# The taps of a depthwise convolution: from split diagonals to plain fp32 products on 32x32 parts of the array

## The chip, the cores and the metric

The kernel runs on one core of one Trainium2 chip. The metric is the device time of one execution in microseconds, given as the median of several runs. The engines are named as the profile names them: PE is TensorE's matmul, PEld its weight load, DVE is VectorE, ACT is ScalarE, POOL is GpSimd, SP is SyncE. A DMA queue is marked by a q behind the engine that issues to it.

## The reference, cut to what matters

A decoder trunk of two layers, 512 tokens by 1024 features, all in float32. Layer 0 has a mixer of state-space groups and attention, layer 1 a convolution module. In both layers a residual, a layer norm, an MLP and another layer norm follow. The change lies in the convolution module of layer 1:

```python
def conformer_conv(x, w_pw1, b_pw1, w_dw, b_dw, ln_g, ln_b, w_pw2, b_pw2):
    h = x @ w_pw1 + b_pw1
    val, gate = jnp.split(h, 2, axis=-1)
    h = val * jax.nn.sigmoid(gate)
    h = lax.conv_general_dilated(                    # depthwise, causal, 31 taps
        h, w_dw[:, None, :], window_strides=(1,), padding=[(CONV_SIZE - 1, 0)],
        dimension_numbers=('NWC', 'WIO', 'NWC'), feature_group_count=CONV_WIDTH) + b_dw
    h = jax.nn.silu(layer_norm(h, ln_g, ln_b))
    return h @ w_pw2 + b_pw2
```

and, around it, `x = layer_norm(alpha * x + mix)`.

## The kernel before

Activations lie with features on the partitions and tokens along the row: a tensor of 1024 features is eight tiles of 128 x 512. The tokens are also cut into two halves of 256 columns (half 0 and half 1), so that a layer norm of one half can run while PE works on the other.

**Products.** A float32 product is made of three products in the type fp32r: both operands are split into a high part and a rest (hi, lo), and hi x hi, hi x lo and lo x hi are summed in PSUM (`gemm`, L219 to L227). The split is one cast on ScalarE and one subtraction on VectorE (`split`, L214 to L217). A few products are plain fp32; each of those shows as two records in the trace, so `colmean` (L873), which makes one product for a mean and four for a variance, shows two records (mpc) and eight (vpc) for each half.

**The convolution stage** (L1041 to L1135) goes through eight tiles of 128 features, j = 0 to 7.
- `glu_tile(j)` makes value and gate (pv and pg, 24 products each; those of tiles 0 and 1, called pl, are made before the stage), the sigmoid on ScalarE (csg), and the gated product on VectorE (hp), behind 30 columns of zeros. hp is split too (hph, hpl).
- `taps_pe(j)` does the first taps on PE: for each tap ScalarE builds two 128 x 128 diagonal matrices from the identity (dh and dl, the hi and lo part of that tap's weights), and PE makes three products of them with a shifted window of hph and hpl, summed in one PSUM bank (cv). PE_TAPS says how many taps: 2, 6, 8, 9, 11, 14 for tiles 0 to 5, and for the halves of tiles 6 and 7 13, 14 and 13, 8.
- `taps_dve(j)` does the other taps: ScalarE opens two sums with the last two taps (cy, cz), and VectorE adds one tap in each step, cy and cz in turn (L1090, recorded as L357). At the end cz and cv are added to cy (recorded as L353).
- `LN.add` sums the tiles as they come (sc, L871); `LN.norm` makes the mean (mpc), subtracts it, squares (sqc on ScalarE), makes the variance (vpc) and its reciprocal root (rc). Then every tile is scaled, passed through Silu and split (csh, csl).
- The tail (`tail_norm_lead`, `Tail`) multiplies the eight split tiles with w_pw2 (tld, 24 products for a half tile), adds the residual and makes the next norm (mpd, vpd). The lead (fl) is the first part of the MLP behind it.

Tiles 6 and 7 are worked in halves, in the order of the list TAIL: P is `taps_pe`, V `taps_dve`, G `glu_tile` for half 1, N the norm of a half; the two digits are tile and half.

**What sets the order.** A scheduler orders the instructions of each engine by the order in which the program makes them and by what is ready, and puts in the semaphores. `tc.add_manual_dep` with NOSYNC fixes the order of two instructions on one engine; in this stage that is used for little. PSUM has six banks for products (`nps`) and two for statistics (`stp`). Weights come through `Weights`: those of the convolution and the tail were split in layer 0 and kept in DRAM, and come back by POOL's DMA queue, each into a slot that waits for PE to have used what is in it; `W.ahead` says how many are asked for in advance.

Of the kernel before, what the change touches and what calls it, by code (L numbers as in the profile page):

```python
# [9 lines left out]
F32 = mybir.dt.float32  # L10
F32R = mybir.dt.float32r
# [154 lines left out]
def kernel(ctx: ExitStack, tc: tile.TileContext, a: dict, out: bass.AP):  # L166
# [639 lines left out]
    def nps(name):  # L806
        return nps_.tile([P, T], F32, tag="n", name=name)
# [7 lines left out]
    def tmp(name, dt=F32):  # L815
        return hid.tile([P, T], dt, tag="tmp", name=name, bufs=8)
# [43 lines left out]
    class LN:  # L860
# [4 lines left out]

        def add(self, j, ys, c0, c1):

            if j == 1:
                self.s[c0] = tmp(f"s{self.n}{c0}")[:, c0:c1]
            if j:  # L870
                (V if j == KT - 1 or self.n in LN_ON_V else G).tensor_tensor(self.s[c0], ys[0][:, c0:c1] if j == 1 else self.s[c0], ys[j][:, c0:c1], op=ALU.add)  # L871

        def colmean(self, srcs, c0, c1, nm, other):  # L873

# [98 lines left out]
            W.fence = None  # L973
            return [ps for _, ps in self.held]

    def tail_norm_lead(xk, name, bias, g, b, lead_n, lead_name):

        ln = LN(name)
        t = Tail(xk, ln, bias)
        t.run(KT)  # L980
# [35 lines left out]
    wdh = hid.tile([P, KT, CONV], F32R, tag="wdh", name="wdh")  # L1016
    wdl = hid.tile([P, KT, CONV], F32, tag="wdl", name="wdl")
# [12 lines left out]
    k0 = 0  # L1030
    for bi, nb in enumerate(FFN_BLOCKS[0]):
# [8 lines left out]

    acc = [None] * KT  # L1041
    hps = [None] * KT
    cps = [None] * KT

    def glu_tile(j, c0=0, c1=T):
        if c0 == 0:
            if j < 2:
                ps[j] = first[2 * j : 2 * j + 2]
            else:
                ws[j], ps[j] = (W.next(), W.next()), (nps(f"pv{j}"), nps(f"pg{j}"))  # L1050
            hps[j] = hpage(f"hp{j}", F32, PAD + T), hpage(f"hph{j}", F32R, PAD + T), hpage(f"hpl{j}", F32R, PAD + T)
# [6 lines left out]
        hp, hh, hl = hps[j]  # L1058
        p0 = PAD + c0 if c0 else 0
# [3 lines left out]
        split(hh[:, p0 : PAD + c1], hl[:, p0 : PAD + c1], hp[:, p0 : PAD + c1])  # L1063

    def taps_pe(j, c0=0, c1=T):
        _, hh, hl = hps[j]
        if c0 == 0:
            cps[j] = nps(f"cv{j}")
        n = PE_TAPS[c0 > 0][j]
        for t in range(n):  # L1070
            dh = hid.tile([P, P], F32R, tag="dh", name=f"dh{j}{t}", bufs=DBUFS)
            dl = hid.tile([P, P], F32R, tag="dl", name=f"dl{j}{t}", bufs=DBUFS)
            act(dh, ident, AF.Copy, scale=wdh.bitcast(F32)[:, j, t : t + 1])
            act(dl, ident, AF.Copy, scale=wdl[:, j, t : t + 1])
            for i, (u, v) in enumerate(((dh, hh), (dh, hl), (dl, hh))):
                PE.matmul(cps[j][:, c0:c1], u, v[:, t + c0 : t + c1], start=t == 0 and i == 0, stop=t == n - 1 and i == 2)  # L1076

    def taps_dve(j, c0=0, c1=T):

        hp = hps[j][0]  # L1080
        if c0 == 0:
            acc[j] = page(f"cy{j}", F32), hpage(f"cz{j}", F32)
        y, z = (x[:, c0:c1] for x in acc[j])
        t = CONV - 1
        act(y, hp[:, t + c0 : t + c1], AF.Identity, bias=pv("conv_b_dw", j), scale=wdw[:, j, t : t + 1])
        t = CONV - 2
        opened = act(z, hp[:, t + c0 : t + c1], AF.Copy, scale=wdw[:, j, t : t + 1])
        for i, t in enumerate(range(CONV - 3, PE_TAPS[c0 > 0][j] - 1, -1)):
            o = (y, z)[i % 2]
            stt(o, hp[:, t + c0 : t + c1], wdw[:, j, t : t + 1], o, ALU.mult, ALU.add)  # L1090
        tt(y, y, z, ALU.add)
        tt(y, y, cps[j][:, c0:c1], ALU.add)
        return opened

    ln = LN("c")
    n = KT - SPLIT_TILES
    cs_, ws, ps = None, [None] * KT, [None] * KT
    glu_tile(0)
    glu_tile(1)
    taps_pe(0)  # L1100
    for j in range(n):
        if j + 2 < KT:
            W.ahead = AHEAD[j + 2 >= n]
            glu_tile(j + 2, 0, T if j + 2 < n else H)
        if j + 1 < n:
            taps_pe(j + 1)
        opened = taps_dve(j)
        if j == 1:
            with tc.issue_after(opened):
                for i in range(KT):  # L1110
                    act(X[i], X[i], AF.Identity, bias=rb[2][:, i : i + 1], scale=ALPHA)
        for c0, c1 in HALVES:
            ln.add(j, [x and x[0] for x in acc], c0, c1)
    for o in TAIL:
        j, (c0, c1) = int(o[1]), HALVES[int(o[-1])]
        if o[0] == "P":
            taps_pe(j, c0, c1)
        elif o[0] == "V":
            taps_dve(j, c0, c1)
            ln.add(j, [x and x[0] for x in acc], c0, c1)  # L1120
        elif o[0] == "G":
            glu_tile(j, H, T)
        else:
            ys = [x[0] for x in acc]
            r = ln.norm(ys, c0, c1)
            cs_ = cs_ or new_x("cs")
            for j in range(KT):
                y = ys[j][:, c0:c1]
                tt(y, y, r, ALU.mult)
                act(y, y, AF.Silu, bias=pv("conv_ln_b", j), scale=pv("conv_ln_g", j))  # L1130
                done = split(cs_[j][0][:, c0:c1], cs_[j][1][:, c0:c1], y)
                if c0 == 0 and j == FJ:
                    W.fence = done
    W.ahead = AHEAD[0]
    xs, first = tail_norm_lead(cs_, "d", None, ("ln1_g", 8), ("ln1_b", 8), LEAD, "fl1")  # L1135


    XT = [None] * KT
# [106 lines left out]
```

## Time and profile before

| | |
|---|---|
| median of 3 runs | 1217.15 us (1216.98 to 1217.62) |
| profiled execution: its own time | 1217.5 us |
| its span in the trace | 1215.8 us |
| granted TensorE clock, mean | 0.995 |
| busy: PE, DVE, ACT, POOL | 98%, 65%, 46%, 5% of the span |
| chain that ended last, by engine | PE 83%, DVE 10%, ACT 4%, DMA 2%, issue 1% |
| convolution stage | about 667 us to 823 us of the span |
| tap products on PE (L1076) | 98 x 3: 150 of 512 columns, 144 of 256 |

The page's first part gives busy time, share of the span and number of instructions of each engine. A view by stretches gives the same for pieces of the span. The chain of waits is followed back from the last instruction: at each step to what released it, or to the instruction before it on its engine; its rows are start, length and what ran, with a count. A group of instructions is written as out<-in with the program's own names, partitions x elements, count, then busy time, mean nanoseconds of one, idle time before them and what ended it. A matmul's duration is longer than the distance to the next, since they are pipelined; the pace is read from the chain, as length over count.

### The profile page before, as it was taken

What the parts mean: (1) busy time and instruction counts of PE and PEld (TensorE: products, weight loads), DVE (VectorE), ACT (ScalarE), POOL (GpSimd) and SP (SyncE); (2) the same over time, 40 slices, a digit from 0 to 9 for tenths busy, and PEclk for the clock granted to TensorE, in tenths of its full rate; (3) what the DMA queues carried; (4) which work ended last, traced back from release to release, by engine and by line L of the source; (5) the groups of instructions that cost most, each with busy time, mean ns of one, the idle gap of its engine ahead of it and who ended that gap; (6) DMA issues with size and microseconds to landing.
All of it is one profiled execution on the core that took longest, in us unless ns stands there. A gap on an engine that the chain in (4) does not pass through costs nothing.

```text
span 1215.8 us, 16751 instructions
## 1 busy us (share of the span) xinstructions
PE 1187.4 (98%) x6546; PEld 1007.5 (83%) x6546; DVE 786.9 (65%) x1400; ACT 557.1 (46%) x990; POOL 58.2 (5%) x125
## 2 busy tenths in 40 slices
PE   9899999999999999999999999899999999999997
PEld 7677776789988888888999888889988888888885
DVE  7998774578745635646566999998843443434446
ACT  6836665734525524425323456964651332323230
POOL 1001101100000000000022110102000000000000
PEclk9999999999999999999999999999999999999999
DMA  8510042150878787887454631406142232323211
GB/s 205 155 49 22 19 130 61 31 195 1 264 250 282 251 284 264 270 283 268 165 183 159 213 104 36 139 1 208 39 152 87 87 108 83 122 70 121 70 52 69
DMA packets 128943, 168.86 MB, mean 139 GB/s; under 512 B 11298, under 2 KB 101666, under 8 KB 128864
## 3 DMA queue, kind: packets, MB, share of 16 engines
q1 hardware_dynamic: 120064, 136.30, 34.5%
q0 software_dynamic: 8640, 31.46, 7.6%
q8 instruction: 51, 0.84, 0.3%
q14 instruction: 28, 0.23, 0.1%
q10 hardware_dynamic: 160, 0.03, 0.0%
HBM read 132.12 MB, written 35.65 MB: 138 GB/s over the span
## 4 chain that ended last, share of the span: by engine, by line
PE 83%; DVE 10%; ACT 4%; DMA 2%; issue 1%; POOL 0%; SPq 0%; DVEq 0%; POOLq 0%; ACTq 0%
PE f L225 23%; PE g L1175 12%; PE acf L225 11%; PE fl L225 5%; PE tld L225 4%; PE tlb L225 4%; PE h L1159 3%; PE cv L1076 2%; PE pv L225 2%; PE pg L225 2%; PE tla L225 2%; PE pl L225 2%; DVE cz L357 1%; PE acmo L225 1%; PE av L709 1%
## 5 line engine op out<-in xcount | busy, mean ns | idle before, releaser
L102 DVE TENSOR_TENSOR wlo<-raw,whi 128x1024 fp32r<-128x1024 f32 x176 | 213.4, 1224 | 199.5 <-ACT whi L101 198.7
L101 ACT CAST whi<-raw 128x1024 fp32r<-128x1024 f32 x176 | 182.1, 1049 | 313.5 <-PE g L1175 107.4
L1175 PE MATMUL g<-whi,hh 128*128 128x512 f32 x208 | 81.8, 393 | 0.0
L1175 PE MATMUL g<-wlo,hh 128*128 128x512 f32 x208 | 81.8, 393 | 0.0
L1175 PE MATMUL g<-whi,hl 128*128 128x512 f32 x208 | 81.7, 393 | 0.0
L225 PE MATMUL f<-xah,whi 128*128 128x512 f32 x208 | 81.2, 390 | 0.0
L225 PE MATMUL f<-xdl,whi 128*128 128x512 f32 x208 | 81.1, 390 | 0.0
L225 PE MATMUL f<-xah,wlo 128*128 128x512 f32 x208 | 81.0, 390 | 0.0
L225 PE MATMUL f<-xdh,whi 128*128 128x512 f32 x208 | 81.0, 390 | 0.0
L225 PE MATMUL f<-xal,whi 128*128 128x512 f32 x208 | 81.0, 390 | 0.0
L225 PE MATMUL f<-xdh,wlo 128*128 128x512 f32 x208 | 81.0, 390 | 0.0
L225 PE MATMUL acf<-hl,whi 128*128 128x512 f32 x192 | 75.7, 394 | 0.0
L225 PE MATMUL acf<-hh,wlo 128*128 128x512 f32 x192 | 75.6, 394 | 0.0
L225 PE MATMUL acf<-hh,whi 128*128 128x512 f32 x192 | 75.5, 393 | 0.0
L215 ACT CAST hh<-fr 128x512 fp32r<-128x512 f32 x64 | 39.7, 621 | 59.6 <-DVE fr L353 59.6
L216 DVE TENSOR_TENSOR hl<-fr,hh 128x512 fp32r<-128x512 f32 x64 | 44.1, 690 | 31.9 <-ACT hh L215 31.8
L357 DVE SCALAR_TENSOR_TENSOR cy<-hp,wdw,cy 128x512 f32<-128x512 f32 (+1 forms) x99 | 63.6, 654 | 0.2
L357 DVE SCALAR_TENSOR_TENSOR cz<-hp,wdw,cz 128x512 f32<-128x512 f32 (+1 forms) x93 | 60.0, 656 | 0.0
L353 DVE TENSOR_TENSOR fr<-fr 128x512 f32<-128x512 f32 x64 | 43.7, 685 | 14.7 <-ACT fr L154 14.6
L1175 PEld LDWEIGHTS g<-wlo,hh 128*128 128x128 f32 x208 | 39.1, 188 | 8.9
L1175 PEld LDWEIGHTS g<-whi,hl 128*128 128x128 f32 x208 | 39.1, 188 | 8.9
L1175 PEld LDWEIGHTS g<-whi,hh 128*128 128x128 f32 x208 | 39.1, 188 | 8.8
(684 smaller groups left out, 3093.4 us busy)
## 6 DMA issues: line engine op xcount, KB each, us to landing
raw<-in_ffn_w_dram SPq DMA_DIRECT2D x48, 1024.0 KB, 5.8
raw<-in_ffn_w_dram SPq DMA_DIRECT2D x32, 512.0 KB, 3.5
kepth<-whi SPq DMA_DIRECT2D x30, 512.0 KB, 8.6
keptl<-wlo SPq DMA_DIRECT2D x30, 512.0 KB, 9.4
whi<-kepth POOLq DMA_DIRECT2D x30, 512.0 KB, 3.7
wlo<-keptl POOLq DMA_DIRECT2D x30, 512.0 KB, 4.5
raw<-in_conv_w_pw_dram SPq DMA_DIRECT2D x12, 1024.0 KB, 6.5
raw<-in_mix_w_in_dram SPq DMA_DIRECT2D x16, 512.0 KB, 3.9
```

The source lines that it names most:

```text
L101: i0 = nc.scalar.copy(hi, raw).ins
L102: i1 = nc.vector.tensor_sub(lo, raw, hi.bitcast(F32)).ins
L215: i0 = S.copy(hi, src).ins
L216: i1 = V.tensor_sub(lo, src, hi.bitcast(F32)).ins
L225: ins = PE.matmul(ps[:, c0:c1], u[:, k, ksl], v[:, c0:c1], start=start and k == 0 and i == 0, stop=stop and k == n - 1 and i == 2).ins
L353: V.tensor_tensor(o, x, y, op=op)
L357: V.scalar_tensor_tensor(o, x, s, y, op0=op0, op1=op1)
L709: ins = PE.matmul(av[R, P * kb :], vt[:, kb, R], ws_[f"{c}{h}"][0][:, o : o + T - P * kb], start=summed[h] == 1, stop=summed[h] == 4, skip ...
L1076: PE.matmul(cps[j][:, c0:c1], u, v[:, t + c0 : t + c1], start=t == 0 and i == 0, stop=t == n - 1 and i == 2)
L1159: PE.matmul(ps, u, v, start=k == 0 and i == 0, stop=k == nk - 1 and i == 2)
L1175: PE.matmul(pss[b], u, v[:, kk, :], start=k + kk == 0 and i == 0, stop=k + kk == nb - 1 and i == 2)
```

## The change

- **Taps on PE.** The split diagonals are gone (dh, dl, hph, hpl). A tap on PE is now plain fp32 on 32 x 32 parts of the array: for each tap four products, one for each group of 32 features, with a 32 x 32 diagonal as weights (`taps_32`). Row group g of the array takes features 32g to 32g + 31, and column strip t mod 4 takes tap t, so that 16 products in a row use 16 different parts. The four row groups write four PSUM banks (cw), in each of which the four strips hold partial sums of every fourth tap. ScalarE copies the four banks to SBUF (cq, `copies`), and `merge` adds the four strips of each group: a plain fp32 product of the 128 x 32 stacked identity (mask) with each cq, four of them into the four strips of a statistics bank (cn).
- **Diagonals.** All diagonals of a tile are made by two multiplications on VectorE, mask times weights, both broadcast (`diagonals`).
- **Who does what.** Tiles 5, 6 and 7 do all 31 taps on PE, tile 2 does 24, tiles 0, 1, 3 and 4 none. VectorE does tiles 0, 1, 3 and 4 in five pieces each (PARTS), and the five that are left of tile 2. Tile 6's value and gate are made in one piece; the taps of tiles 6 and 7 are still made by halves.
- **Order.** CONV_ORDER lists the steps: d diagonals, g value and gate, v a piece of VectorE's taps, p taps on PE, c copies, m merge, f the end of a tile with taps on PE, x the scaling of X for the residual, N and n the norm of a half, with the steps between them placed ahead of its variance. `in_order` ties each instruction of PE, VectorE and ScalarE in the stage to the one before it on its engine. After the first norm the tail's first product group runs (AHEAD_OF_REST), then the rest of the list.
- Within the norm, the split of a tile is now written behind the scaling of the next one. `LN.add` starts its sum from whatever tile comes first.

```diff
-PE_TAPS = ((2, 6, 8, 9, 11, 14, 13, 14), (10, 10, 10, 10, 10, 10, 13, 8))
-TAIL = "P60 P70 V60 V70 G61 G71 N0 P71 P61 V61 V71 N1".split()
-DBUFS = 6
-SPLIT_TILES = 2
+PE_TAPS = ((0, 0, 24, 0, 0, 31, 31, 31), (0, 0, 0, 0, 0, 0, 31, 31))
+PARTS = 5
+AHEAD_OF_REST = 1
+CONV_ORDER = "d2 g0 g1 v0 g2 v0 v0 g3 v0 p2 v1 c2 v0 v1 x0 v1 g4 v1 m2 f2 v1 v3 g5 d5 v3 g6 v3 v3 d7 p5 c5 d6 m5 f5 v3 g70 v4 p60 c60 v4 v4 v4 p70 c70 g71 m60 f60 m70 f70 v4 p61 c61 N0 p71 m61 n0 f61 c71 m71 f71 N1 n1".split()
+SPLIT_TILES = 1
...
-        V.tensor_copy(wdh, wdw)
-        V.tensor_sub(wdl, wdw, wdh.bitcast(F32))
+        tt(mask, ident[:, :32], ident[:, 32:64], ALU.add)
+        tt(mask, mask, ident[:, 64:96], ALU.add)
+        tt(mask, mask, ident[:, 96:], ALU.add)
...
-            for i, (u, v) in enumerate(((dh, hh), (dh, hl), (dl, hh))):
-                PE.matmul(cps[j][:, c0:c1], u, v[:, t + c0 : t + c1], start=t == 0 and i == 0, stop=t == n - 1 and i == 2)
...
+    def part_of(t, g):
+        return slice(32 * g, 32 * g + 32), slice(32 * (t % 4), 32 * (t % 4) + 32)
+
+    def taps_32(j, c0=0, c1=T):
+
         n = PE_TAPS[c0 > 0][j]
+        if not n:
+            return
+        if not Ds[j]:
+            diagonals(j)
+        cps[j, c0] = [nps(f"cw{j}{c0}{g}")[:, c0:c1] for g in range(4)]
         for t in range(n):
+            for g in range(4):
+                R, C = part_of(t, g)
+                PE.matmul(cps[j, c0][g][C, :], Ds[j][t // 16][R, t % 16, :], hps[j][R, t + c0 : t + c1], start=t < 4, stop=t >= n - 4,
+                          tile_position=(R.start, C.start))
+
+    def diagonals(j):
+        most = max(PE_TAPS[0][j], PE_TAPS[1][j])
+        Ds[j] = [hpage(f"D{j}{i}", F32, T).rearrange("p (t c) -> p t c", c=32) for i in range(-(-most // 16))]
+        for i, D in enumerate(Ds[j]):
+            m = min(16, most - 16 * i)
+            V.tensor_tensor(D[:, :m], mask.unsqueeze(1).broadcast_to([P, m, 32]),
+                            wdw[:, j, 16 * i : 16 * i + m].unsqueeze(2).broadcast_to([P, m, 32]), op=ALU.mult)
+
+    def copies(j, c0=0, c1=T):
+        qs[j, c0] = [hpage(f"cq{j}{c0}{g}", F32, T)[:, c0:c1] for g in range(4)]
+        for q, ps_ in zip(qs[j, c0], cps[j, c0]):
+            S.copy(q, ps_)
+
+    def merge(j, c0=0, c1=T):
+
+        cps[j, c0] = stp(f"cn{j}{c0}")[:, c0:c1]
+        for g in range(4):
+            PE.matmul(cps[j, c0][32 * g : 32 * g + 32, :], mask, qs[j, c0][g], start=True, stop=True, tile_position=(0, 32 * g))
...
+    def in_order(at):
+
+        for ins in traced[at:]:
+            if ins.engine in (PE.engine, V.engine, S.engine):
+                if ins.engine in queue:
+                    tc.add_manual_dep(ins, queue[ins.engine].name, NOSYNC, reason="order of the convolution")
+                queue[ins.engine] = ins
...
+        r = ln.norm(ys, c0, c1, (None, others if between else None))
...
+        for j in range(KT):
+            y = ys[j][:, c0:c1]
+            tt(y, y, r, ALU.mult)
+            if j:
+                out(j - 1)
+            act(y, y, AF.Silu, bias=pv("conv_ln_b", j), scale=pv("conv_ln_g", j))
+        out(KT - 1)
...
+    def the_rest(t):
+        at = len(traced)
+        t.run(AHEAD_OF_REST)
+        in_order(at)
+        run(CONV_ORDER[split_at:])
```

More of the change, by code (lines that the diff above doesn't have):

```diff
@@ L1015 @@
     wdw = hid.tile([P, KT, CONV], F32, tag="wdw", name="wdw")
-    wdh = hid.tile([P, KT, CONV], F32R, tag="wdh", name="wdh")
-    wdl = hid.tile([P, KT, CONV], F32, tag="wdl", name="wdl")
+    mask = hid.tile([P, 32], F32, tag="mask", name="mask")
     def taps():
@@ new lines, in merge, with taps_dve @@
+    def merge(j, c0=0, c1=T):
+        cps[j, c0] = stp(f"cn{j}{c0}")[:, c0:c1]
+        for g in range(4):
+            PE.matmul(cps[j, c0][32 * g : 32 * g + 32, :], mask, qs[j, c0][g], start=True, stop=True, tile_position=(0, 32 * g))
+    def taps_dve(j, c0=0, c1=T, part=0, parts=1):
+        hp, n = hps[j], PE_TAPS[c0 > 0][j]
+        if c0 == 0 and part == 0:
+            acc[j] = page(f"cy{j}", F32), hpage(f"cz{j}", F32) if n < CONV else None
+        y, z = (x and x[:, c0:c1] for x in acc[j])
+        if n == CONV:
+            act(y, cps[j, c0], AF.Identity, bias=pv("conv_b_dw", j))
+            return
+        if part == 0:
+            t = CONV - 1
+            act(y, hp[:, t + c0 : t + c1], AF.Identity, bias=pv("conv_b_dw", j), scale=wdw[:, j, t : t + 1])
+            t = CONV - 2
+            last["opened"] = act(z, hp[:, t + c0 : t + c1], AF.Copy, scale=wdw[:, j, t : t + 1])
+        todo = list(enumerate(range(CONV - 3, n - 1, -1)))
+        for i, t in todo[len(todo) * part // parts : len(todo) * (part + 1) // parts]:
@@ L1089, in taps_dve @@
             o = (y, z)[i % 2]
             stt(o, hp[:, t + c0 : t + c1], wdw[:, j, t : t + 1], o, ALU.mult, ALU.add)
-        tt(y, y, z, ALU.add)
-        tt(y, y, cps[j][:, c0:c1], ALU.add)
-        return opened
+        if part == parts - 1:
+            tt(y, y, z, ALU.add)
+            if n:
+                tt(y, y, cps[j, c0], ALU.add)
     ln = LN("c")
     n = KT - SPLIT_TILES
[L1097 to L1112, printed above, removed]
-            ln.add(j, [x and x[0] for x in acc], c0, c1)
@@ L1114 @@
[L1114 to L1118, printed above, removed]
+    ws, ps, last = [None] * KT, [None] * KT, {}
+    Ds, part, cs_ = [None] * KT, [0] * KT, []
+    queue, traced = {}, nc.cur_bb.bb.instructions
+    def in_order(at):
[4 more added lines that the diff above has]
+                queue[ins.engine] = ins
@@ new lines, in scaled_x, with add, norm_half, others @@
+    def scaled_x():
+        for i in range(KT):
+            act(X[i], X[i], AF.Identity, bias=rb[2][:, i : i + 1], scale=ALPHA)
+    def add(j, halves):
+        for c0, c1 in halves:
+            ln.add(j, [x and x[0] for x in acc], c0, c1)
+    def norm_half(h, between):
+        c0, c1 = HALVES[h]
+        ys = [x[0] for x in acc]
+        def others():
+            for o in between:
+                step(o)
+            return next(i for i in reversed(traced) if i.engine == PE.engine)
+        r = ln.norm(ys, c0, c1, (None, others if between else None))
+        cs_[:] = cs_ or new_x("cs")
+        done = {}
+        def out(j):
+            y = ys[j][:, c0:c1]
+            done[j] = split(cs_[j][0][:, c0:c1], cs_[j][1][:, c0:c1], y)
+        for j in range(KT):
+            y = ys[j][:, c0:c1]
+            tt(y, y, r, ALU.mult)
[3 more added lines that the diff above has]
+        out(KT - 1)
+        if c0 == 0:
+            W.fence = done[FJ]
@@ L1119, with step @@
+    def step(o):
+        k, j, (c0, c1) = o[0], int(o[1]), HALVES[int(o[2])] if len(o) > 2 else (0, T)
+        if k == "g":
+            W.ahead = AHEAD[j >= n]
+            glu_tile(j, c0, c1)
+        elif k == "p":
+            taps_32(j, c0, c1)
+        elif k == "d":
+            diagonals(j)
+        elif k == "c":
+            copies(j, c0, c1)
+        elif k == "m":
+            merge(j, c0, c1)
+        elif k == "x":
+            scaled_x()
+        elif k == "f":
             taps_dve(j, c0, c1)
-            ln.add(j, [x and x[0] for x in acc], c0, c1)
-        elif o[0] == "G":
-            glu_tile(j, H, T)
-        else:
[L1124 to L1133, printed above, removed]
+            add(j, ((c0, c1),) if len(o) > 2 else HALVES)
+        else:
+            part[j] += 1
+            taps_dve(j, 0, T, part[j] - 1, PARTS)
+            if part[j] == PARTS:
+                add(j, HALVES)
@@ new lines, in run @@
+    def run(order):
+        between = None
+        for o in order:
+            if o[0] == "N":
+                between = []
+            elif between is not None and o[0] != "n":
+                between.append(o)
+            else:
+                at = len(traced)
+                if o[0] == "n":
+                    norm_half(int(o[1]), between)
+                    between = None
+                else:
+                    step(o)
+                in_order(at)
+    split_at = CONV_ORDER.index("n0") + 1
@@ L1134 @@
+    run(CONV_ORDER[:split_at])
+    def the_rest(t):
+        at = len(traced)
+        t.run(AHEAD_OF_REST)
+        in_order(at)
+        run(CONV_ORDER[split_at:])
     W.ahead = AHEAD[0]
[L1135 removed]
+    xs, first = tail_norm_lead(cs_, "d", None, ("ln1_g", 8), ("ln1_b", 8), LEAD, "fl1", the_rest)
     XT = [None] * KT
```

51 lines of the change are left out of this document (18 added, 33 removed).

## The prediction

> **What bounds the kernel now.** I read the page's engine line first, then the stage in stretches, then the chain of waits through it. The columns of the second fence are stretch, length, then busy time of each engine with its instructions, granted clock, DMA share and GB/s.
>
> ```profile
> PE 1187.4 (98%) x6546; PEld 1007.5 (83%) x6546; DVE 786.9 (65%) x1400; ACT 557.1 (46%) x990; POOL 58.2 (5%) x125
> ```
>
> ```profile
> 667.00:743.00 76.00, 76.00 (x357) 63.37 (x357) 75.33 (x122) 40.76 (x102) 9.53 (x18) 1.00 0.44 149
> 743.00:783.00 40.00, 35.95 (x263) 34.04 (x261) 39.66 (x83) 31.76 (x96) 4.22 (x8) 1.00 0.31 105
> 783.00:796.00 13.00, 10.82 (x58) 9.36 (x58) 12.60 (x36) 12.20 (x35) 0.00 (x0) 0.87 0.02 6
> 796.00:823.00 27.00, 27.00 (x218) 26.69 (x218) 25.03 (x70) 15.31 (x39) 0.00 (x0) 1.00 0.01 2
> ```
>
> ```profile
> 655.23 12.00 PE pl L225 x96
> ...
> 705.70 5.45 PE pg L225 x24
> 711.15 6.26 PE cv L1076 x27
> ...
> 748.15 0.60 DVE cy L353
> 748.74 0.66 DVE cz L357
> 749.40 0.67 DVE sc L871 x2
> ...
> 779.93 0.40 DVE cy L357
> ...
> 783.30 1.22 PE mpc L879 x2
> ...
> 790.32 0.36 ACT rc L160
> 790.69 1.28 ACT L156
> ...
> 795.48 5.46 PE tld L225 x42
> ...
> 817.13 1.73 PE vpc L879 x8
> ...
> 852.17 5.75 PE fl L225 x48
> ```
>
> PE carries the whole kernel, so only two things count: products that leave PE, and time in which PE waits. In the convolution PE and VectorE are both full until 743. From 743 the chain lies on VectorE's tap steps (cy, cz), up to the mean of half 0 (mpc, 783.30). PE has nothing to do meanwhile, and waits again until the first product of the tail (tld, 795.48). This row shows the longest gap:
>
> ```profile
> 782.81 0.39 PE L1076 MATMUL cv<-hph,dh 128*128 128x256 f32 x1 [4.05 <-ACT hph L215]
> ```
>
> In 667 to 823 PE busy falls short of the time by 6.2 us, and in the 13 us after that gap the granted clock is 0.87. From 796 on PE is full again: whatever brings 795.48 forward is worth its full length, as long as nothing behind it turns late.
>
> **Prices.** From the chain, length over count: a split product of 512 columns 5.45/24 = 0.227 us in the GLU and 6.26/27 = 0.232 in the taps; of 256 columns 5.75/48 = 0.120; a plain fp32 product of 256 columns has two records, 1.73/8 = 0.216 us each. A VectorE tap step follows the last by 0.66 us (512) or 0.40 (256); an add of 512 by 0.60, of 256 by 0.335. The rows below give mean durations, longer than the pace because neighbours overlap:
>
> ```profile
> L357 DVE SCALAR_TENSOR_TENSOR cy<-hp,wdw,cy 128x512 f32<-128x512 f32 x64 | 46.5, 746 | 0.2
> L357 DVE SCALAR_TENSOR_TENSOR cz<-hp,wdw,cz 128x512 f32<-128x512 f32 x60 | 44.6, 749 | 0.0
> L357 DVE SCALAR_TENSOR_TENSOR cy<-hp,wdw,cy 128x256 f32<-128x256 f32 x35 | 17.1, 488 | 0.0
> L357 DVE SCALAR_TENSOR_TENSOR cz<-hp,wdw,cz 128x256 f32<-128x256 f32 x33 | 16.1, 487 | 0.0
> L216 DVE TENSOR_TENSOR hpl<-hp,hph 128x542 fp32r<-128x542 f32 x6 | 4.3, 721 | 0.8 <-ACT hph L215 0.7
> ```
>
> ```profile
> L154 ACT ACTIVATE dh<-ident,wdh 128x128 fp32r<-128x128 f32 x92 | 36.0, 391 | 6.4 <-PE cv L1076 6.3
> L154 ACT ACTIVATE dl<-ident,wdl 128x128 fp32r<-128x128 f32 x92 | 35.7, 388 | 0.0
> L215 ACT CAST hph<-hp 128x542 fp32r<-128x542 f32 x6 | 3.8, 638 | 1.7 <-DVE hp L357 1.7
> L160 ACT ACTIVATE csg<-pg,PV 128x512 f32<-128x512 f32 x4 | 2.7, 684 | 24.9 <-PE pg L225 24.9
> ```
>
> **Removed.** From PE 294 tap products: 50 taps x 3 at 0.232 and 48 half taps x 3 at 0.120, together 52 us. From ScalarE 196 diagonal builds (71.7 us of busy time in the 184 of the rows) and ten casts. From VectorE the tap steps fall from 124 of 512 and 68 of 256 (109 us by pace) to 121 of 512 (80 us), and the hpl splits (5 us) go.
>
> **Added on PE: the one price that the trace lacks.** A tap becomes four products of 32x32, eight records. The nearest row is L528, plain fp32 on 128 rows by 32 columns, four column strips with 128, 96, 64 and 32 columns:
>
> ```profile
> L528 PE MATMUL tp<-Cx,Gx x256: 195/246/419, 55.1 to 146.4; 128*32 128x64 f32 x43, 128*32 128x128 f32 x34, 128*32 128x32 f32 x28, 128*32 128x96 f32 x23
> ```
>
> ```profile
> 112.13 1.93 PE L528 MATMUL tp<-Cx,Gx 128*32 128x128 f32 x64
> 113.99 0.38 PE L540 MATMUL vR<-U,gt 128*128 128x128 f32 x1
> ```
>
> 64 records from 112.13 to 113.99: 0.029 us each with the switches at both ends. One after another at 0.216 per 256 columns they would need 16 x (128+96+64+32) x 0.216/256 = 4.3 us; the longest strip alone needs 16 x 0.108 = 1.73. So four strips stream side by side, each at the pace of the full array, and a switch costs about 0.1 us. Lower bound: 16 parts do the same. Then a record of 512 columns costs 0.43/16 = 0.027 us and one of 256 columns 0.0135. Upper bound: the four row groups take turns and only the strips overlap, 0.107 and 0.054. I take 0.027 at 512, which L528 sustained over 64 records, because row groups read different partitions. At 256 columns 0.0135 would be twice the rate seen; I take 0.020, between that and L528's. So p2 (24 taps, 192 records) costs 5.1 + 0.2, p5 (248) 6.6 + 0.2, each half block of tiles 6 and 7 (248) 5.0 + 0.2. The merges: four strips of 512 columns side by side, 0.86 us a tile, four tiles' worth 3.4.
>
> No run here shows row groups side by side; the Trainium skill, "TensorE: Matmul & The Clock Gate", section "Measured speedup vs the span model", states 10.6x for 16 parts, and by it the lower bound would be the better one.
>
> PE's work thus falls from 52 to about 37 us (5.3 + 6.8 + 4 x 5.2 + 3.4 + switches). That alone isn't the gain, since VectorE was the late one.
>
> **The order, walked through.** The diff ties each engine to the written order, so a gate that is late holds all behind it on VectorE.
> - PE ends pl at 655.23 + 12.00 = 667.2. hp1 comes after the sigmoid, so VectorE begins v0 at about 669.4 and has five steps until 672.7. Next in its order stands hp2, whose gate leaves PE at 667.2 + 10.9 = 678.1 and ScalarE at 679.0: VectorE waits 6.3 us. Twelve steps later it waits 2.3 us for hp3 (PE 689.0) and is at 690.5.
> - From there to the mean of half 0 it has 104 tap steps (68.8), gates 4 to 7 (2.8), diagonals 5, 6, 7 (two multiplies of about 0.6 each, 3.6; not in the trace, priced as an add of 512), six whole adds (3.6) and twelve half sums (4.0): 82.8, so 773.4.
> - PE meanwhile: p2 to 694.3, g4, m2 706.2, g5, g6 728.0; waits for diagonal 5 (VectorE 730.6); p5 737.5; the four copies of c5 stand between p5 and m5 with nothing behind them in PE's order, 2.4 us at 0.6 (as hph); m5 740.8, g70 746.6, p60 751.8; 0.9 us until a bank is copied out; p70 757.8, g71 763.6, m60 and m70 764.6, p61 769.7. VectorE is later by 3.7, so it sets the mean: 773.5 instead of 783.3.
> - p71 and m61 then stand before the variance on PE: 773.9 + 5.2 + 0.5 + 1.73 = 781.3. From the reciprocal root over the table load to the first tail product it took 795.48 - 790.32 = 5.2 us before, with diagonals in between on ScalarE; without those I estimate 4.1. First tail product 785.4, 10.1 us earlier.
> - Behind it: p71 holds four of six banks until its copies, which ScalarE makes only after the eight silus, so PE runs two outputs at a time (0.7 us lost), waits 0.9 for m71, and after a wait of 4 us the clock is granted late again (before, 0.13 x 13 = 1.7 us): 3.1 lost. Of the old stage 19 tap products (2.3) ran after 795.48, of the new one m71 (0.5).
>
> Sum: 10.1 - 3.1 + 2.3 - 0.5 = 8.8 us. Half 1's split tiles are ready by about 812 and half 0's tail ends near 814 (785.4 + 192 x 0.12 + statistics 2.2 + 0.5 + 3.1), so nothing there turns late; the lead and the last layer are untouched. ScalarE's copies cost no path beyond c5 and the bank, as it loses over 70 us of diagonals; the eight scalings of X (x0) now stand before g4's sigmoid, whose operand PE has only at 705, some 4 us later. The mask costs three small adds on VectorE in place of a copy and a subtraction, in layer 0's MLP. The pw2 weights are queued behind PE's own slots as before, with a DMA share of 0.31 in the rows of 743 to 783. The profiled run has 1217.5 us around a span of 1215.8; the median is 1217.15. Against the median: **1208.3**.
>
> **Rivals.** (1) PE can't issue small records that fast. L528 shows 64 in a row; if half lay ready and only the others show the rate, it is 1.86/32 less the switches, 0.052. Then p61 ends about 802, the walk has PE late instead of VectorE, and the tail starts near 822: +27, about 1245. It decides from 0.032 per record on, where the tail starts at 794.1 and the net loss of 1.3 behind it eats the rest. For it: no block as long as 248 records; against: four blocks of L528 ran without thinning out. The Trainium skill's "TensorE: Matmul & The Clock Gate", section "Wait — 56ns, not 53.3ns?", names 62 ns per matmul for a sequencer that decodes in microcode; by that the walk would end near 1260, and L528's 29 ns speaks against it on these 64. (2) Row groups take turns, the upper bound: tail at 848, 1271. Against it only that their partitions differ. (3) Half blocks cost L528's 0.027: PE is late by 1.5, tail at 788.9, about 1212. (4) Fixed order costs at hand-overs: some 60 steps change engine, and 0.15 us more at each eats the 9: 1217. For it: the gates of tiles 1 to 3 already stop VectorE for 12 us, which the free order of before filled. (5) VectorE loses less at those gates than I walk, PE's 0.0135 holds, the mean comes at 768 and the tail near 779: 1202.
>
> **How the numbers follow.** Forecast 0.52 (its own range 1204 to 1211, by the half-block price from 0.0135 to 0.025), rival 1 0.14, rival 2 0.05, rival 3 0.13, rival 4 0.09, rival 5 0.07. Faster by over 0.2% (2.4 us, about what a measurement of this kernel tells from no change): forecast, 3 and 5, 0.72. Within: rival 4 less a little, 0.08. Slower: 1, 2 and a rest of 4, 0.20. The range runs from rival 5 to a mild form of rival 1, 0.036 per record: 1202 to 1224.
>
> **What would show it.** Right: p5 takes some 6.8 us, a half block 3.5 to 5.5; VectorE waits for the sigmoids of tiles 1 to 3; mpc of half 0 near 773 with sc or cy of tile 4 as its releaser; tld from about 785, then PE full. Wrong: records of cw more than 0.031 us apart (rival 1), or in fours (rival 2); gaps on VectorE between tap steps of one part (rival 4). If mpc is early but tld isn't, the stretch between variance and tail is mispriced.

## The result and the profile after

The changed kernel takes 1209.85 us (median, 1209.02 to 1211.38), the kernel before took 1217.07 in the same series: ratio 0.9941, 95% interval 0.9928 to 0.9953. The forecast was 1208.3, 8.8 us less than before; it became 7.2. The profiled execution has 1211.38 us around a span of 1209.7 (before 1217.5 and 1215.8).

The engine line of the page after, then the first three of the four stretches shown before (columns as there):

```profile
PE 1179.6 (98%) x7684; PEld 986.1 (82%) x7684; DVE 752.2 (62%) x1313; ACT 500.5 (41%) x802; POOL 58.2 (5%) x125
```

```profile
667.00:743.00 76.00, 73.99 (x702) 54.62 (x701) 66.59 (x107) 18.88 (x31) 11.51 (x22) 1.00 0.50 173
743.00:783.00 40.00, 36.65 (x1115) 27.61 (x1114) 35.15 (x65) 10.97 (x27) 2.11 (x4) 1.00 0.17 56
783.00:796.00 13.00, 9.53 (x53) 8.51 (x51) 8.18 (x21) 10.58 (x23) 0.00 (x0) 0.74 0.01 1
```

VectorE, full before until 783, is now idle for 9.4 us of the first stretch, and ScalarE works 29.9 us instead of 72.5 in the first two. But PE, too, falls short: 8.8 us in the first three stretches, and in the third its clock is 0.74. So the change made room on all engines, and little of it is used. The chain of waits through the stage (start, length, what):

```profile
730.21 8.67 PE cw L1084 x235
...
768.05 5.24 PE cw L1084 x215
...
774.45 0.67 PE mpc L884 x2
775.12 3.25 PE cw L1084 x135
...
781.46 1.94 PE vpc L884 x8
...
783.42 0.48 ACT rc L161
...
786.85 8.38 PE tld L226 x46
...
845.25 0.43 PE mpd L884 x2
```

The mean of half 0 (mpc) comes at 774.45 instead of 783.30, the first tail product (tld) at 786.85 instead of 795.48: 8.6 us earlier. At the second mean of the next normalisation (the last row; 851.74 before) 6.5 us are left, and the span is 6.1 shorter. A little of this lead was there ahead of the stage. The last variance before it starts at these times, first in the kernel before, then in the changed one:

```profile
650.50 1.74 PE vpb L879 x8
```

```profile
649.91 1.74 PE vpb L884 x8
```

Counted from that row, the mean comes 8.3 us earlier, the first tail product 8.0, and 5.9 are left at the last row. In the traces below this start lies up to 2.5 us away from the changed kernel's before the stage has begun; where it matters, times are given counted from it as well. VectorE's waits for the sigmoids of tiles 2 and 3 are where the walk had them; the last field is the wait and its releaser:

```profile
678.14 0.75 DVE L358 SCALAR_TENSOR_TENSOR hp<-pv,PV,csg 128x512 f32<-128x512 f32 x1 [6.48 <-ACT csg L161]
689.01 0.75 DVE L358 SCALAR_TENSOR_TENSOR hp<-pv,PV,csg 128x512 f32<-128x512 f32 x1 [2.14 <-ACT csg L161]
```

### The profile page after: what moved, and what is told of

Same layout as the page of the kernel before. It is cut to its first block, busy times and chain, and to the rows that moved or that the text cites. A ratio compares the mean times of both kernels' runs of the same rounds, so it can differ in the third digit from the quotient of the medians.

```text
span 1209.7 us, 18684 instructions
## 1 busy us (share of the span) xinstructions
PE 1179.6 (98%) x7684; PEld 986.1 (82%) x7684; DVE 752.2 (62%) x1313; ACT 500.5 (41%) x802; POOL 58.2 (5%) x125
## 4 chain that ended last, share of the span: by engine, by line
PE 79%; DVE 11%; DMA 4%; ACT 3%; issue 2%; POOL 0%; SPq 0%; DVEq 0%; ACTq 0%; POOLq 0%
PE f L226 20%; PE g L1268 12%; PE acf L226 10%; PE fl L226 5%; PE tld L226 4%; PE tlb L226 3%; DMA raw<-in_ffn_w_dram 3%; PE h L1252 3%; PE cw L1084 3%; DVE wlo L103 2%; PE pl L226 2%; DVE cy L358 1%; PE pv L226 1%; PE pg L226 1%; DVE cz L358 1%
## 5 line engine op out<-in xcount | busy, mean ns | idle before, releaser
L226 PE MATMUL acf<-hl,whi 128*128 128x512 f32 x192 | 75.4, 393 | 0.0
L226 PE MATMUL acf<-hh,wlo 128*128 128x512 f32 x192 | 75.4, 393 | 0.0
L358 DVE SCALAR_TENSOR_TENSOR cy<-hp,wdw,cy 128x512 f32<-128x512 f32 x63 | 47.0, 749 | 0.0
L226 PEld LDWEIGHTS f<-xah,wlo 128*128 128x128 f32 x208 | 39.0, 188 | 8.2
```

The lines of the kernel that those rows point to most:

```text
L226: ins = PE.matmul(ps[:, c0:c1], u[:, k, ksl], v[:, c0:c1], start=start and k == 0 and i == 0, stop=stop and k == n - 1 and i == 2).ins
L358: V.scalar_tensor_tensor(o, x, s, y, op0=op0, op1=op1)
```

## The experiments

Ratios are to the kernel before, in the same series of runs; that of the changed kernel is 0.9941.

### Which products stand side by side

```diff
-        for t in range(n):
-            for g in range(4):
+        for g in range(4):
+            for t in range(n):
```

> The loop over row groups stands outside the loop over taps, so up to 31 products in a row stay in one row group; the sums are the same. Theory (records side by side in different row groups are what makes 0.0325 us per record of 512 possible): inside one row group only the four column strips overlap, as in the block of L528, so a record costs 0.43/4 = 0.107 us at 512 and 0.054 at 256; p2 (192 records) takes 20.6 us in place of 6.0, p5 (248) 26.6 in place of 8.0, each half block some 13.3 in place of 5 to 6.5; the mean of half 0 comes near 828 and the kernel takes about 1270. Rival (the pace is set by how fast PE's queue hands out records, whatever their place): the blocks keep 0.0325 and 0.020 to 0.026 and the time stays within 1207 to 1213.

Measured, in a single execution: 1316.04 us, 98 above the kernel before (1218.23 in that series). The blocks in the chain, p2 and p5 of this kernel:

```profile
687.29 25.44 PE cw L1084 x192
...
748.76 39.07 PE cw L1084 x243
```

Stretches inside p5 of this kernel, and below them p5 of the changed kernel:

```profile
749.00:752.00 3.00, 3.00 (x32) 0.88 (x28) 3.00 (x6) 0.55 (x1) 0.89 (x2) 1.00 0.62 218
...
757.00:768.00 11.00, 11.00 (x74) 2.58 (x70) 5.47 (x9) 1.17 (x2) 0.00 (x0) 0.50 0.00 1
768.00:787.00 19.00, 19.00 (x108) 4.24 (x100) 0.00 (x0) 0.59 (x2) 0.00 (x0) 0.50 0.00 1
```

```profile
730.20:738.30 8.10, 8.10 (x248) 5.11 (x248) 8.10 (x14) 0.00 (x0) 0.00 (x0) 1.00 0.38 131
```

In the changed kernel 248 records take 8.10 us, 0.0327 each, at full clock. With one row group at a time 32 records take 3.00 us at full clock in the first of these stretches, 0.094 each; then the granted clock falls to 0.50 and a record costs 0.15 to 0.18. Over the whole blocks the mean granted clock is 0.61 in p2 and 0.57 in p5; with the lengths weighted by it a record costs 0.081 and 0.090 us, an estimate, somewhat less than the 0.107 expected. The rival, a pace set by PE's queue alone, is out: the same instructions in another order cost 4 to 5 times as much. But each row group also writes a PSUM bank of its own, so this run can't tell neighbours in one row group from neighbours in one bank. That the clock falls was in neither theory, and is why 1316 lies above the 1270 expected, since at full clock the records are cheaper than expected, not dearer.

### VectorE's waits at the gates

```diff
-d2 g0 g1 v0 g2 v0 v0 g3 v0 p2 v1 c2 v0 v1 x0 v1 g4 v1 m2 f2 v1 v3 g5
+d2 g0 v0 g1 v0 v0 v0 g2 v0 v1 v1 g3 v1 p2 v1 c2 v1 x0 g4 m2 f2 v3 g5
```

> Only the written order of VectorE's pieces changes: pieces of tiles 0 and 1 stand ahead of the gates of tiles 2 and 3, so VectorE no longer stops for the sigmoids (4.5, 6.5 and 2.1 us in the changed kernel). Theory (VectorE's last half sum at 774.3 sets the mean, and PE, done with p61 at 773.2, is 1.2 us behind it): VectorE is through some 10 us earlier, PE becomes the last by its own length, the mean comes 1.2 to 2.5 us earlier (also by the 1.3 us that PE waits for diagonal 5), and the time is 1.5 to 2.5 us below that of the changed kernel, about 1207.7, ratio to the kernel before 0.992. Rival (VectorE alone is the bound and PE's blocks have slack): the mean comes near 764 and the time near 1200, ratio 0.986. Second rival (a VectorE that fills its waits delays hp2 and hp3 and with them PE): no gain, 1210.

Measured: 1209.38 us, ratio 0.9928 (0.9913 to 0.9944): by the ratios 1.6 us less than the changed kernel, the size that the theory gave, though the two intervals overlap. VectorE's waits for sigmoids in the stage, first the changed kernel, then this one (total, count, longest):

```profile
DVE hp L358 <- ACT csg L161: 15.3, 5, 6.5
```

```profile
DVE hp L358 <- ACT csg L161: 11.5, 5, 5.0
```

Only 3.8 us went: VectorE, early now, waits at the next gates, the last of them the second half of tile 7's, behind which the last piece of tile 4 is written. That gate and the last sums on VectorE, in the changed kernel:

```profile
767.59 0.48 DVE L358 SCALAR_TENSOR_TENSOR hp<-pv,PV,csg 128x256 f32<-128x256 f32 x1 [0.21 <-ACT csg L161]
...
773.88 0.76 DVE L354 TENSOR_TENSOR sc<-sc,cy 128x256 f32<-128x256 f32 x2
```

The same in this kernel, then the copies that the profile names as the mean's releaser, and the mean in the chain:

```profile
767.96 0.48 DVE L358 SCALAR_TENSOR_TENSOR hp<-pv,PV,csg 128x256 f32<-128x256 f32 x1 [2.22 <-ACT csg L161]
...
774.25 0.76 DVE L354 TENSOR_TENSOR sc<-sc,cy 128x256 f32<-128x256 f32 x2
```

```profile
773.88 1.20 ACT L1098 COPY cq<-cw 128x256 f32<-128x256 f32 x4 [4.84 <-PE cw L1084]
```

```profile
774.82 0.67 PE mpc L884 x2
```

The mean starts at 774.82, before the last copy ends (773.88 + 1.20 = 775.08), so the last copy can't have released it. Of the two sums the mean of half 0 needs the first; a sum takes 0.42 us, so it ended at 774.67, 0.15 us ahead of the mean, as in the changed kernel (773.88 + 0.42 = 774.30, mean at 774.45). So VectorE's last sum still releases the mean. But from tile 7's gate to the mean both kernels take 6.86 us, and at that gate VectorE waits for PE, 0.21 us in the changed kernel and 2.22 here: the two engines were tied there already, and now PE sets when VectorE may begin its last piece. What the edit moved is PE, which works 75.4 of the 76 us of the first stretch instead of 74.0. The variance ahead of the stage starts at 652.45 in this trace; counted from it the mean comes 2.2 us earlier than in the changed kernel, within the 1.2 to 2.5 of the theory. PE did become the limit, though ahead of VectorE's last piece and not behind it.

### PE's work between mean and tail

First p71 alone moved behind the variance, ahead of the first tail product (T marks that product's place; the changed kernel has it right behind n0):

```diff
-p61 c61 N0 p71 m61 n0 T f61 c71 m71 f71 N1 n1
+p61 c61 N0 m61 n0 p71 T f61 c71 m71 f71 N1 n1
```

> Only the place of the block p71 changes: it stands behind the variance of half 0 on PE instead of ahead of it, still ahead of the first tail product. In the changed kernel PE ran the mean at 774.45, p71 to 780.5, the variance at 781.46 to 783.40, then waited 3.5 us for the first normalised tile, and from 783 to 796 the granted clock was 0.74. Theory (the block delays the variance, and the wait behind it costs the clock): the squares are summed at 779.3, so the variance ends near 779.6, the first normalised tile is there at 783.0, PE is busy with p71 until about 785.2 and goes on with the tail without a wait, at a clock above 0.9: first tail product 785.2 instead of 786.85, and 2 to 3 us less lost at a low clock, together 3.5 to 5 us, about 1205.5, ratio 0.9905. Rival (the variance wasn't held up by p71, or the products that follow wait for VectorE's and ScalarE's tiles in any case): the first tail product stays within 0.5 us of 786.85 and the time within 1 us of 1209.85. Second rival (p71's four banks, free only after the copies, now stop the tail's outputs): slower than 1210.

Measured: 1211.13 us, ratio 0.9944 (0.9928 to 0.9959): no gain. The variance in the chain, and p71 in the order of time:

```profile
779.17 2.75 PE vpc L884 x8
```

```profile
781.83 6.01 PE L1084 MATMUL cw<-hp,D 32*32 32x256 f32 x248
787.78 0.39 PE L226 MATMUL tld<-csh,whi 128*128 128x256 f32 x1
```

The variance does start 2.3 us earlier (3.7 counted from the variance ahead of the stage, which starts at 651.31 in this trace), and the wait of 3.5 us behind it is gone. But PE now waits 2.6 us ahead of the variance instead, and the low clock has moved with the wait: it is 0.50 from 780.5 to 783.5 (0.97 in the mean from 783 to 796), and the products of the variance take 2.75 us instead of 1.94. p71 holds the first tail product back to 787.78, but the chain doesn't lie on p71. From 784.28 to 791.94 it lies on ScalarE, which needs 0.94 us for the Silu and the cast of each of the eight tiles:

```profile
790.97 0.51 ACT cy L161
791.50 0.41 ACT csh L216
```

The work filled one hole by leaving another, and behind the holes ScalarE's tiles are the next limit. Counted from the variance ahead of the stage, the second mean of the next normalisation comes 2.0 us earlier in this trace; the ratio shows no such gain, and with an interval of 0.0016 to either side (1.9 us) it can't exclude one either.

Then the second half of tile 7's gate as the filler of that other hole:

```diff
-p70 c70 g71 m60 f60 m70 f70 v4 p61 c61 N0 p71 m61 n0 T f61 c71 m71 f71
+p70 c70 m60 f60 m70 f70 v4 p61 c61 N0 g71 m61 n0 p71 T f61 c71 m71 f71
```

> Of that new order only the last part, in the order of the changed kernel: the second half of tile 7's gate moves from ahead of p61 to between mean and variance of half 0 on PE, and p71 behind the variance. VectorE keeps its waits at the gates. Theory (VectorE sets the mean, so PE only waits in another place): mean near 773.7 instead of 774.45, PE waits about 5 us ahead of it, no gain: 1208.5 to 1211, ratio 0.993 to 0.995. Rival (PE's idle time and its low clock between mean and tail are what is lost, 3.5 us of waits and 0.26 x 13 us of clock): about 1204 to 1205, ratio 0.990.

Measured: 1213.3 us, ratio 0.9962 (0.9947 to 0.9978), no gain, and by the ratios some 2.6 us worse than the changed kernel, with intervals that just overlap. Its wait ahead of the mean, and then the mean and tile 7's value in the chain:

```profile
PE mpc L884 <- DVE sc L354: 5.0, 1, 5.0
```

```profile
774.90 1.19 PE mpc L884 x2
776.09 3.64 PE pv L226 x24
```

As the theory had it, the wait only moved to where VectorE is late: 5.0 us ahead of the mean. What it had left out is the price of it: after that wait the mean's product takes 1.19 us instead of 0.67, and the 24 value products 3.64; the 24 gate products behind them, without a wait ahead, take 2.88.

Both partial edits together:

```diff
-d2 g0 g1 v0 g2 v0 v0 g3 v0 p2 v1 c2 v0 v1 x0 v1 g4 v1 m2 f2 v1 v3 g5
+d2 g0 v0 g1 v0 v0 v0 g2 v0 v1 v1 g3 v1 p2 v1 c2 v1 x0 g4 m2 f2 v3 g5
...
-p70 c70 g71 m60 f60 m70 f70 v4 p61 c61 N0 p71 m61 n0 T f61 c71 m71 f71
+p70 c70 m60 f60 m70 f70 v4 p61 c61 N0 g71 m61 n0 p71 T f61 c71 m71 f71
```

> The two partial edits together, with the rest of the changed kernel's order: VectorE's first pieces ahead of the late gates, and the second half of tile 7's gate and p71 as PE's work between mean, variance and tail; the last piece of tile 4 no longer stands behind that gate. Alone the first gave a ratio of 0.9928, the second 0.9962, against 0.9941 for the changed kernel, that is -1.6 and +2.6 us. Theory (each only moves the wait to the other engine; together VectorE can be early and PE has work that may wait): more than the sum of the two; the walk gives a mean of 769.4 (773.5 for the changed kernel) and 4.3 us less, about 1205.5, ratio 0.990. Rival (they add up): 1 us slower than the changed kernel, about 1211, ratio 0.995.

Measured: 1208.15 us, ratio 0.9916 (0.9901 to 0.9931). Adding the two would give 0.9949, above that interval; so they seem to help each other, if by less than the walk had; the sum is itself uncertain by some 0.0025. The mean:

```profile
769.30 1.19 PE mpc L884 x2
```

It is where the walk put it (769.4), 5.1 us earlier than in the changed kernel. But PE waits 2.1 us ahead of it and then runs slow again (1.19), and the first tail product comes at 785.90, behind p71: of 5.1 us about 1 arrives there. From 782.09 the chain lies on ScalarE's eight tiles again. Behind the tail's start PE keeps full clock, where the changed kernel has 0.74 until 796.

### The order as such

```diff
-            if ins.engine in (PE.engine, V.engine, S.engine):
+            if ins.engine in ():
```

> The changed kernel with the same split of taps and the same text order, only that nothing ties the three engines to it: the scheduler chooses. Theory (the written order isn't itself the gain, its stops at the gates of tiles 1 to 3 cost VectorE 13 us, and the scheduler's order fills them but strews PE's blocks and merges between the GLU's products): within 4 us of the changed kernel, 1206 to 1214. Rival (the fixed order is what earns the change, as the run with the parts alone suggests): 1220 or more.

Measured: 1216.62 us, ratio 0.9991 (0.9976 to 1.0006), between the two expectations. Waits of VectorE and PE in the stage, and the mean:

```profile
DVE sc L354 <- ACT cy L155: 17.5, 3, 12.2
```

```profile
PE cw L1084 <- DVE hp L358: 5.8, 1, 5.8
```

```profile
780.61 0.63 PE mpc L884 x2
```

Free, the scheduler fills the gates of tiles 1 to 3 (VectorE works 71.2 us instead of 66.6 until 743), but it leaves tile 5's gate so late that p5 waits 5.8 us for it, and VectorE then waits 17.5 us for tiles that come through p5, p60 and p70. The new split without the ties of the written order (the program's text still stands in it) is worth nothing that can be measured.

### The cheap product as such

The old split of the taps with 32x32 products in the old loops, once as the scheduler orders it, once with VectorE's steps tied to take turns between their two accumulators:

```diff
-                PE.matmul(cps[j][:, c0:c1], u, v[:, t + c0 : t + c1], ...)   # three split products per tap
+                PE.matmul(cw[g][C, :], Ds[j][R, t, :], hps[j][R, t + c0 : t + c1], ...)   # four parts per tap
+        q = [hpage(...) for g in range(4)]        # copies, then the merge by mask
...
+        for one, two in zip(steps, steps[1:]):    # the second kernel alone
+            tc.add_manual_dep(two, one.name, NOSYNC, reason="taps by turns")
```

> The kernel before, with its split of the taps between PE and VectorE, its pace of two tiles ahead and its free order, only that PE's taps are 32x32 products in plain fp32 with copies and merges instead of three split products per tap (tile 0 has four taps on PE instead of two). PE saves about 52 - 13.5 - 10 - 6.9 = 22 us, VectorE loses the splits (5 us) and two tap steps and gains the diagonal multiplies (about 8), ScalarE loses over 70 us of diagonals. Theory (in the kernel before VectorE's own work sets the mean of half 0, at 783.3, so work taken from PE alone isn't seen): the mean stays at 782 to 786 and the time at 1215 to 1220, ratio 0.998 to 1.003; the gain of the change comes from moving taps from VectorE to the cheap products. Rival (PE's 22 us are what the change earns): about 1197, ratio 0.984.

> As the run with the parts alone (the kernel before, its split of taps and free order, PE's taps as 32x32 products), only that VectorE's tap steps of a tile are tied to take turns between the two accumulators, as they did in the kernel before. In the run with the parts alone the free order put all steps on one accumulator first, 0.79 us from step to step in place of 0.66. Theory (this is what made the parts alone slower than the kernel before): 192 steps get 0.13 us shorter, the mean of half 0 comes back by some 20 us, and the time is 1215 to 1224. Rival (it was PE: merges in PE's queue that wait for copies and for VectorE, and small products strewn between the GLU's, cost the 24 us): it stays at 1236 to 1244.

Measured: 1241.94 us, ratio 1.0200 (1.0178 to 1.0223), and 1242.1, ratio 1.0199 (1.0178 to 1.0219). The first theory falls: less work on PE made the kernel 24 us slower, not equal. The second falls as well: with turns VectorE's steps are 0.66 us apart again, and nothing is gained. Waits of VectorE and PE in the second kernel, and its first stretch:

```profile
DVE hp L356 <- ACT csg L159: 20.2, 4, 14.5
...
PE mpc L878 <- DVE sc L870: 9.8, 1, 9.8
PE cn L1086 <- DVE cy L352: 5.9, 3, 3.2
```

```profile
667.00:743.00 76.00, 69.11 (x494) 41.79 (x496) 56.04 (x91) 21.40 (x36) 8.62 (x17) 0.96 0.39 132
```

VectorE stands idle for 20 us of the first stretch, waiting for sigmoids, once for 14.5 us, while merges in PE's queue wait for VectorE's adds (5.9). It does the half steps of tiles 6 and 7 that the mean needs from 791 to 805, the mean comes at 806.4, and PE waits 9.8 us for it. In the first kernel VectorE was busy (69.9 of 76 us) at its slower pace; the end is the same. What both share is an order that nobody had walked for these products; that this is the cause isn't shown, and the next run speaks against it as the whole of it.

Then the old split in the new kernel's code, in a written order found by walking the prediction's prices:

```diff
-PE_TAPS = ((0, 0, 24, 0, 0, 31, 31, 31), (0, 0, 0, 0, 0, 0, 31, 31))
+PE_TAPS = ((4, 6, 8, 9, 11, 14, 13, 14), (0, 0, 0, 0, 0, 0, 13, 8))
-CONV_ORDER = "d2 g0 g1 v0 g2 v0 v0 g3 v0 p2 ..."
+CONV_ORDER = "d5 g0 d4 d6 d0 v0 p0 v0 d1 g1 c0 v0 d3 v1 ..."
```

> The split of the taps as in the kernel before (4, 6, 8, 9, 11, 14, 13 and 14 taps on PE, 8 in the second half of tile 7, 13 in that of tile 6, the rest on VectorE), PE's taps as 32x32 products with copies and merges, all three engines in a written order found by the same walk as the new one. It tells the cheap product and the written order from the move of taps. Theory (the gain is in the taps that the cheap products let move from VectorE to PE; without that move VectorE's 122 whole and 68 half steps set the mean, whatever the order): mean of half 0 not before 778, and the time by the walk 14 us above the changed kernel's, 1218 to 1226, ratio 1.000 to 1.007. Rival (the written order with cheap products earns it by itself, and the two runs with the parts alone were slow for their free order alone): 1212 or less, ratio below 0.996.

Measured: 1235.03 us, ratio 1.0139 (1.0116 to 1.0162). PE's longest wait, and the mean:

```profile
PE cn L1104 <- DVE cy L354: 11.5, 2, 6.7
```

```profile
789.38 0.68 PE mpc L884 x2
```

The rival is out: cheap products in a written order don't earn it with the old split. The walk was too kind by 9 us, counted from the slow end of its range: with taps of every tile on both engines each tile has a merge, and these wait for VectorE's adds in PE's queue. Only one order of this split was tried; a better one may exist.

### Everything walked anew

```diff
-d2 g0 g1 v0 g2 v0 v0 g3 v0 p2 v1 c2 v0 v1 x0 v1 g4 v1 m2 f2 v1 v3 g5 d5 v3 g6 v3 v3 d7 p5 c5 d6 m5 f5 v3 g70 v4 p60 c60 v4 v4 v4 p70 c70 g71 m60 f60 m70 f70 v4 p61 c61 N0 p71 m61 n0 T f61 c71 m71 f71 N1 n1
+g0 d5 v0 v0 v0 g1 v0 v1 v0 d2 g2 g3 v1 v3 v1 g4 p2 v1 c2 v3 d6 v4 v3 v4 g5 m2 f2 v1 g6 v4 p5 v3 c5 x0 d7 v4 g70 v4 p6 c6 m5 p70 f5 m6 v3 c70 m70 f6 f70 N0 g71 n0 p71 T c71 m71 f71 N1 n1
```

> The same products and tap steps as the changed kernel, only in another written order, found by walking the prediction's prices through with the measured ones in place (0.0325 us a record of 512, 0.0225 of 256; by these the walk gives a mean of 773.5 for the changed kernel, measured 774.45): VectorE starts with four pieces of tile 0 and no longer stands before a gate whose product isn't there; tile 6's taps go as one block of 512 columns; the second half of tile 7's gate stands between mean and variance of half 0 on PE, and p71 between variance and tail, so that PE has work in both waits. Theory (in the changed kernel VectorE's waits at the gates delay the mean, and PE then has nothing to do between mean and tail, so both have to be cured together): the mean of half 0 comes at 762 to 764 instead of 774.45, the first tail product at about 776 instead of 786.85, the second mean of the next normalisation near 832 instead of 845.25, and the time is 1197 to 1199, ratio 0.984. Rival (the tail is bound by its weights' transfers, or by half 1, so that an earlier mean turns into a later wait): the mean comes at 763 but the tail has gaps, and the time stays above 1204. Second rival (each hand-over written down costs more than walked): mean at 768 or later, above 1203.

Measured: 1198.37 us, ratio 0.9835 (0.9815 to 0.9854), faster than both kernels, 11.5 us below the changed one. VectorE's waits for sigmoids, the stretches, and the chain:

```profile
DVE hp L358 <- ACT csg L161: 4.1, 2, 2.2
```

```profile
667.00:743.00 76.00, 76.00 (x731) 58.48 (x731) 75.73 (x123) 16.44 (x27) 11.63 (x22) 1.00 0.52 177
...
783.00:796.00 13.00, 13.00 (x103) 12.74 (x102) 9.88 (x29) 9.09 (x19) 0.00 (x0) 1.00 0.01 1
```

```profile
744.03 8.56 PE cw L1084 x228
...
762.60 0.70 PE mpc L884 x2
...
833.16 0.43 PE mpd L884 x2
```

The mean is at 762.60, the first tail product at 777.06 and the second mean of the next normalisation at 833.16 (expected 762 to 764, about 776 and near 832), and the third stretch runs full at full clock. Tile 6 as one block takes 8.56 us (744.03) where its two half blocks of the changed kernel, 5.8 and 5.2 in the chain, took 11.0. PE shows no wait in the tail, for weights or for half 1, and the mean lies well below the 768 of the second rival: both rivals are out. From 773.22 to 780.86 the chain lies on ScalarE's tiles here too. No run tells apart what earns the 10 us by which this order beats both partial edits together. The trace does show that those edits had left most of VectorE's waits in place: until 743 VectorE works 75.7 of 76 us here, 67.8 with both edits.

## Why the prediction was right, point by point

**The bound.** That VectorE's last sum releases the mean of half 0, and that an earlier mean comes through to the end, held in the changed kernel (774.45, the sum ended at 774.30), in the two runs where PE was given its work elsewhere and waited for the sum, and in the new order, where a mean 11.9 us earlier (12.5 counted from the variance ahead of the stage) became 11.5 us of time. That PE's holes are worth their length didn't hold as such: with p71 in the hole of 3.5 us no gain could be measured.

**VectorE's walk.** Waits of 6.3 and 2.3 us were walked, 6.48 and 2.14 came; the mean was walked to 773.5 and came at 774.45. Counted from the start of the stage it is 1.5 us late, since the trace that the walk starts from begins the stage 0.6 later. Some 1.1 of this are sums: a whole add took 0.70 us where 0.60 was priced (six of them), a half sum 0.38 where 0.335 was (twelve).

**The record price: the term that was mis-sized.** At 512 columns 0.027 us was taken, and p5 has 0.0327 (8.10/248); in the chain it takes 8.67 us instead of 6.8. At 256 columns 0.020 was taken, and the four half blocks were priced at 20.8 us. Here are p60 and p70 of the changed kernel in the chain:

```profile
747.97 3.97 PE cw L1084 x177
751.93 0.38 issue
752.31 1.41 PE cw L1084 x53
...
754.12 1.97 PE cw L1084 x64
...
759.06 0.71 issue
759.77 1.33 PE cw L1084 x44
```

p60 goes from 747.97 to 753.72, 5.8 us, p70 from 754.12 to 761.10, 7.0; p61 took 5.24 (above), p71 5.8 (775.12 to 780.89): 23.7 together. That is 0.021 to 0.028 a record. Part of it are holes that the profile calls issue, without a wait that it could show (0.38 in p60, 0.9 in p70, 0.4 in p71); their cause stays open. Thus rival 3 (0.027) was half true. Of rival 1 the sign came in the wide blocks (0.0327 is more than 0.031 apart), but not the reason: at 256 columns the same queue handed out p61's records 0.021 apart, so the queue didn't set the 0.0327, and what did stays open. PE's p61 ended at 773.3 instead of 769.7, so the cover of 3.7 us under VectorE, from which the dearer records were paid, was used up: at tile 7's last gate VectorE already waits 0.21 us for PE. That the mis-sized records cost the mean almost nothing is luck of just this size; dearer ones would have moved it. A record of a full plain fp32 product takes 0.216 us at 256 columns (1.73/8), so the gain of the 16 parts is 7.7 to 10.3 there, and about 13 at 512 columns (an estimate, with twice 0.216 for the full record). The Trainium skill ("TensorE: Matmul & The Clock Gate", section "Measured speedup vs the span model") states 10.6x for 16 parts. The narrow blocks here stay below that figure and the wide ones above it.

**Mean to tail.** The variance was to end at 781.3 and ended at 783.40: 0.95 us by the later mean, the rest by p71, dearer too, and a slower variance. The stretch to the tail was estimated at 4.1 and took 3.4 (783.42 to 786.85). Tail 785.4 walked, 786.85 measured.

**Behind the tail's start.** A net loss of 1.3 us was predicted and 2.1 came (8.6 us of lead, 6.5 left): the clock in the 13 us after the wait was 0.74, not the 0.87 of before that the estimate had carried over. Counted the prediction's way that is 3.4 us instead of 1.7, so other terms must have come out cheaper; which ones isn't shown. The prediction's own three losses there (0.7, 0.9 and 1.7) also add up to 3.3, not to the 3.1 of its sum, which should have given 8.6.

**The step that failed.** The written order was weighed as a cost alone (rival 4: its gates stop VectorE, which the free order of before filled). The runs show both sides. It does stop VectorE, and a better one is worth another 11.5 us; but without its ties the new split is at 0.9991. The old split with cheap products is at 1.014 to 1.020 in a free or a written order. So the 7 us belong to the new split and the written order together, and the prediction's sum has no term for what the order earns.

## What to carry to other kernels

When two engines are nearly tied, an edit for one engine's waits, or one that fills the other's, mostly moves the wait to the next gate and gains little; walk both through with measured prices and cure them together. When times of two traces are compared, count them from a row ahead of the change. A written order is worth what its walk is worth: every piece placed behind a gate waits for it, and work that can wait belongs into the holes that stay, such as those between a mean, its variance and what is normalised by it. Where small products are packed on one array, set the loops so that neighbours in the queue lie in different row groups (and, as here, write different banks), and keep the blocks wide.

## What the runs showed of the hardware

- 32x32 products whose neighbours lie in the same row group and PSUM bank cost 0.08 to 0.09 us a record of 512 columns at full clock (0.094 in the stretch shown), well over twice the 0.0327 of those that go through the row groups by turns; and with PE busy without a hole the granted clock then falls to 0.50 for as long as that lasts (757 to 787 in p5, and likewise in p2), while it stays at 1.00 in p5 of the mixed order.
- After a wait of 5.0 us on PE the next 24 value products took 3.64 us instead of 2.88, at a granted clock of 0.50 until 777.5. Even after 2.6 us (with another wait of 1.3 shortly before it) eight records of the variance took 2.75 instead of 1.94; after the 1.26 us ahead of the changed kernel's mean the clock stayed at 1.00.
- VectorE steps that add to the same accumulator one after another follow each other by 0.78 to 0.79 us, those that take turns between two by 0.66 (in the chain of the first run with the parts alone, steps on cz start at 735.53, 736.31 and 737.10).
